# Layer A's products in the wide form, c spread by DMA, layer B's tokens in the order of t mod 4

## The chip, the cores and the metric

The kernel runs on one core of one Trainium2 chip. The metric is the time of one execution in microseconds on the device; the time of a kernel is the median of several executions. One execution of each kernel is also profiled: the profile gives every instruction of the five engines (PE for matmuls, PEld for the loads of PE's weights, DVE for vectors, ACT for activations, POOL for general work) and the transfers, which SP issues.

## The reference, cut to what matters

One sequence of 256 tokens (L), width 2048 (D), two layers. Layer A is a Mamba-2 mixer, layer B an attention over dilated windows. All inputs are float32.

```python
def reference(x, c, ada_w, ...):
    for layer in range(2):
        shift, scale, gate = split(silu(c) @ ada_w[layer] + ada_b[layer], 3)
        h = x * (1.0 + scale) + shift
        if layer == 0:            # layer A
            z, xBC, dt = split(h @ a_in_w, [4096, 4096 + 6144])
            xBC = silu(causal_conv4(xBC) + conv_b)
            xs, B, C = split(xBC)           # 64 heads of 64, 8 groups of 128
            y = ssd(xs, softplus(dt + dt_bias), A, B, C) + xs * D_skip
            y = rms_norm_by_group(y * silu(z)) * norm_g
            y = y @ a_out_w
        else:                     # layer B
            q, z = split(h @ b_in_w, [3072])
            for g, (window, dilation) in enumerate(((128, 1), (512, 4), (2048, 16))):
                # query t sees t, t - dilation, ..., t - window; ALiBi; 8 heads of 128
                o[g], lse[g] = attention(q[g], k_sh[g], v_sh[g])
            o = sum(o[g] * softmax(lse)[g]) * silu(z)
            y = o @ b_out_w
        x = layer_norm(2 ** 0.5 * x + (1 + gate) * y) * ln_g[layer] + ln_b[layer]
        if layer == 0:
            k_sh, v_sh = split(x @ kv_w, 2)
    return x
```

## The kernel before, in words

**Products.** Every weight comes as pieces of 128x1024 floats (512 KB, load_piece, L88, six buffers). A piece is split into two numbers of the type fp32r: ACT copies it (whi, L94), and DVE subtracts the copy from it (wlo, L95). The activations are split in the same manner into a high and a low part. A product is then high times high, high times low and low times high, all added up in PSUM.

There are three forms. In the *quad* form (cm_piece, L109 to L121) the result has the columns of the weight in its partitions: for each of the 16 blocks of 128 rows of the weight (kt) and each of four blocks of columns PE runs three matmuls over 256 tokens, L119, L120 and L121. In the *wide* form (cm_wide, L140) the high and the low activations lie side by side, so L151 multiplies the weights' high part with both at once over 512 columns, and L152 multiplies the low part with the high activations over 256. The result has two halves, joined by an ACT copy (L156) and a DVE add (L157). The third form (tm_piece, tm_mults, L172 to L174) has the tokens in the partitions and runs three matmuls over 512 columns of weight. Layer A's xs, B and C use the quad form, z the third; layer B's queries and part of its keys use the wide one.

**The start.** The two rows of c come by DMA into the tiles of z (sz, L415), PE multiplies them with a column of ones to spread them over the 128 partitions (L422), and ACT applies SiLU into cb_ (L423). The 96 columns of the modulation (scale, shift and gate of two layers, 16 blocks each) are tiles of 128x2048 (1 MB, ada_load, L230), and each is one DVE instruction, a product with cb_ that is summed along the row (ada_dot, L236). Once scale and shift of a block kt are there, ACT makes h of this block (L381, L382) and DVE its low part. The table of rows at L392 sets how the products that use the h blocks made so far stand between the blocks: seven pieces a row and two or four blocks h. Products begun here and finished later keep a partial sum in the tiles of y and sz (part).

**Layer A.** product (L326) computes xs, B and C by cm_quad, adds a partial sum if there is one (L344), and runs the causal convolution (conv, L298 to L307), which reads PSUM or the partial sum: one ACT instruction with bias and scale (L302), three DVE instructions (L305) and SiLU. stage1, stage2 and stage3 (from L528) do the scan of one group of heads each. The out projection, the residual and the layer norm follow (L657 to L699).

**Layer B.** x_tiles (L707) transposes the normed rows into xhi and xlo, the layer's activations; key and value products follow. u, the residual, is then multiplied with the layer norm's weight and given its bias by POOL (L766, L767), in 16 instructions of 128x512. attend (L785) runs for each of eight heads and two blocks b of 128 queries: three score matmuls, one a group (L795), with 128 keys for the first block and 256 for the second, the mask and slope by DVE (L797, L799), the softmax over all three groups together, transposes (L809), copies (L813, L815) and the products with the values (L819, L820). split_act (L841) splits the result for the last product.

**What sets the order.** The program is written in the order of the code and then re-ordered by a planner (price, graph, build, forward, backward, arrange): it has a price for every instruction and the transfers, works out when each could run, and writes each engine's queue anew, the issues on SP too. So the order on an engine is not that of the code.

Of the kernel before, what the change touches and what calls it, by code (L numbers as in the profile page):

```python
# [24 lines left out]
G = 8  # L25
# [21 lines left out]
CD, CA, NBIAS = 0, 256, 256 + 768  # L47
# [3 lines left out]
def trunk(ctx, tc, xT, x, c, par, cst, bias, lnrow, ada, wdt, win, wout, wkv, wk1, wbin, wbout, out):  # L51
    nc = tc.nc
    V, S, T, PO = nc.vector, nc.scalar, nc.tensor, nc.gpsimd
# [79 lines left out]
    def cm_quad(src, ahi, alo, rate=(0, 1), k0=0):  # L133
        ps = acc_pair()
        for q in range(k0 // 2, KT // 2):
            cm_piece(src, q, ps, ahi, alo, k0=k0)
            background(*rate)
        return ps

    def cm_wide(src, dst, rate=(0, 1)):  # L140


        ps = acc_pair()
        for q in range(KT // 4):
            hi, lo = (t.rearrange("p k n -> p (k n)").rearrange("p (k n) -> p k n", k=4)
                      for t in split(load_piece(src[q])))
            for k in range(4):
                kt = 4 * q + k
                for n in range(2):
                    c_ = slice(n * P, n * P + P)  # L150
                    T.matmul(ps[n], hi[:, k, c_], xp[:, kt], start=kt == 0, stop=False, skip_group_check=True)  # L151
                    T.matmul(ps[n][:, 0, :], lo[:, k, c_], xhi[:, kt, :], start=False, stop=kt == KT - 1,  # L152
                             skip_group_check=True)
            background(*rate)
        for n in range(2):
# [72 lines left out]
    def ada_load(pool, layer, kind, ct):  # L228
        raw = pool.tile([P, D], F32, name="araw", bufs=2)
        nc.sync.dma_start(raw, ada[layer, KIND.index(kind), ct])  # L230
        return raw

    def ada_dot(layer, kind, ct, raw):

        j = KIND.index(kind)
        V.scalar_tensor_tensor(raw, raw, 1.0, cb_, op0=ALU.mult, op1=ALU.mult,  # L236
                               accum_out=mod[layer][:, ct, j:j + 1])
# [31 lines left out]
    hp = act.tile([P, 2, KT, L], F32R, name="actT")  # L269
    hhi, hlo = hp[:, 0], hp[:, 1]  # L270

    with ExitStack() as cA:
# [14 lines left out]
        with ExitStack() as cS:  # L287
# [38 lines left out]
            def product(kind, g, pre=None):  # L326
# [13 lines left out]
                ps = cm_quad(src, hhi, hlo, rate=R, k0=k0)  # L340
                t = tiles(ps)
                if part is not None:
                    for w in range(2):
                        V.tensor_tensor(part[:, 2 * w:2 * w + 2, :], ps[w], part[:, 2 * w:2 * w + 2, :], op=ALU.add)  # L344
                    t = [part[:, n, :] for n in range(4)]
# [5 lines left out]
            with ExitStack() as c0:  # L351
# [68 lines left out]
                for i in range(4):  # L420
                    pc = mm.tile([P, 512], F32, name="acc")
                    T.matmul(pc, ones[:1, :], szt[i // 2][:1, i % 2, :], start=True, stop=True)  # L422
                    S.activation(cb_[:, 512 * i:512 * i + 512], pc, AF.Silu)  # L423
# [210 lines left out]
        def y_tiles(g):  # L634

            for i in range(4):
                ct = 4 * g + i
                if i % 2 == 0:
                    pt = aux.tile([P, 512], F32, name="aux").rearrange("p (i l) -> p i l", i=2)
                for b in range(2):  # L640
                    T.transpose(pt[:, i % 2, b * P:b * P + P], y[g][:, b, i * P:i * P + P], ident)
                w, hi = pv("normg")[:, ct:ct + 1], yhi[g // 4][:, ct % 16, :]
                S.activation(hi, pt[:, i % 2, :], AF.Copy, scale=w)
                V.scalar_tensor_tensor(ylo[g][:, i, :], pt[:, i % 2, :], w, hi.bitcast(F32),
                                       op0=ALU.mult, op1=ALU.subtract)
# [776 lines left out]
```

## Time and profile before

| | us |
|---|---|
| median of three executions | 1287.76 (1283.16 to 1289.54) |
| profiled execution | 1281.55 |
| span of its instructions | 1279.8 |
| granted TensorE clock in it, mean | 0.993 |

The span runs from the first to the last instruction of the profiled execution. Where the profile gives a group of instructions, the row has the line of the kernel, the engine, the operation and its tiles (out<-in), the shape, the count, the busy time and the mean of one, and behind the last bar the idle time of the engine just before them with what ended it. An engine's idle time costs nothing unless something else waits for it in turn.

### The profile page before, as it was taken

To read this page: it belongs to the slowest core of one execution; us is meant where nothing else is said; L and a number is where in the kernel's file an instruction comes from. 1 tells how busy PE (TensorE), PEld (TensorE's weight loads), DVE (VectorE), ACT (ScalarE), POOL (GpSimd) and SP (SyncE) were. 2 spreads that over 40 slices of the span, in tenths; PEclk is the share of its full clock that TensorE was granted. 3 is DMA by queue.
4 is the path that set the end of the run, shared out by engine and by line. 5 is a ranking of instruction groups with operands and counts; after the bars stand their busy time and mean duration, and the time that the engine had idled before them with its cause. 6 is when DMAs were issued, how large, how long until landed. Compare 5 with 4: busy or idle time off the path is not lost.

```text
span 1279.8 us, 19378 instructions
## 1 busy us (share of the span) xinstructions
PE 1239.4 (97%) x7386; PEld 1095.2 (86%) x7386; DVE 1039.2 (81%) x1457; ACT 696.6 (54%) x1027; POOL 33.3 (3%) x20
## 2 busy tenths in 40 slices
PE   6999999999999999999999899999999999999995
PEld 4978999899899999788888699888888888888884
DVE  6999978999998887978895799998745647848778
ACT  4644566868577767764333444444445645444551
POOL 0000000000000000000000135000000000000000
PEclk9999999999999999999999899999999999999998
DMA  9999967887785556578997688999866663453571
GB/s 372 422 422 422 384 216 268 314 276 247 240 300 191 173 159 203 162 258 269 400 376 218 222 315 308 396 420 395 299 191 193 211 185 115 147 183 107 155 266 66
DMA packets 80449, 334.82 MB, mean 262 GB/s; under 512 B 9090, under 2 KB 9314, under 8 KB 67684
## 3 DMA queue, kind: packets, MB, share of 16 engines
q1 hardware_dynamic: 80356, 333.58, 73.5%
q8 instruction: 58, 0.95, 0.3%
q14 instruction: 35, 0.29, 0.1%
HBM read 331.37 MB, written 2.18 MB: 261 GB/s over the span
## 4 chain that ended last, share of the span: by engine, by line
PE 78%; DMA 12%; DVE 7%; ACT 1%; issue 1%; SPq 0%; DVEq 0%; ACTq 0%
PE acc L151 12%; PE acc L174 11%; PE acc L173 11%; PE acc L172 11%; PE acc L152 6%; DMA raw<-in_win 6%; PE acc L119 6%; PE acc L121 6%; PE acc L120 6%; DMA araw<-in_ada 5%; DVE wlo L95 2%; PE py L589 1%; DVE araw L236 1%; PE aux L795 1%; PE po L819 1%
## 5 line engine op out<-in xcount | busy, mean ns | idle before, releaser
L95 DVE TENSOR_TENSOR wlo<-raw,whi 128x1024 fp32r<-128x1024 f32 x395 | 488.9, 1244 | 176.5 <-ACT whi L94 175.2
L94 ACT ACTIVATE whi<-raw 128x1024 fp32r<-128x1024 f32 x395 | 417.1, 1057 | 382.1 <-PE acc L174 178.6
L119 PE MATMUL acc<-actT,whi 128*128 128x256 f32 x960 | 273.6, 288 | 11.8 <-ACT actT L382 7.4
L173 PE MATMUL acc<-wlo,actT 128*128 128x512 f32 x704 | 276.4, 393 | 0.6 <-DVE wlo L95 0.6
L172 PE MATMUL acc<-whi,actT 128*128 128x512 f32 x704 | 274.8, 393 | 1.6 <-ACT whi L94 1.0
L121 PE MATMUL acc<-actT,wlo 128*128 128x256 f32 x960 | 270.5, 285 | 1.4 <-DVE wlo L95 1.4
L120 PE MATMUL acc<-actT,whi 128*128 128x256 f32 x960 | 271.3, 285 | 0.0
L151 PE MATMUL acc<-actT,whi 128*128 128x512 f32 x704 | 251.3, 398 | 0.0
L236 DVE SCALAR_TENSOR_TENSOR araw<-araw,cb__72 128x2048 f32<-128x2048 f32 x96 | 218.4, 2286 | 9.0 <-DMA araw<-in_ada 5.7
L152 PE MATMUL acc<-actT,wlo 128*128 128x256 f32 x704 | 201.8, 287 | 0.6 <-DVE wlo L95 0.6
L119 PEld LDWEIGHTS acc<-actT,whi 128*128 128x128 f32 x960 | 185.2, 194 | 15.7 <-ACT actT L382 9.0
L121 PEld LDWEIGHTS acc<-actT,wlo 128*128 128x128 f32 x960 | 184.0, 193 | 2.3 <-DVE wlo L95 2.0
L120 PEld LDWEIGHTS acc<-actT,whi 128*128 128x128 f32 x960 | 185.1, 193 | 0.3
L174 PE MATMUL acc<-whi,actT 128*128 128x512 f32 x448 | 175.1, 391 | 0.0
L172 PEld LDWEIGHTS acc<-whi,actT 128*128 128x128 f32 x704 | 131.9, 188 | 30.1 <-ACT whi L94 2.8
L151 PEld LDWEIGHTS acc<-actT,whi 128*128 128x128 f32 x704 | 132.2, 188 | 29.2
L173 PEld LDWEIGHTS acc<-wlo,actT 128*128 128x128 f32 x704 | 132.3, 188 | 27.5 <-DVE wlo L95 1.1
L152 PEld LDWEIGHTS acc<-actT,wlo 128*128 128x128 f32 x704 | 133.0, 189 | 1.9 <-DVE wlo L95 1.2
L174 PE MATMUL acc<-whi,ylo 128*128 128x512 f32 x256 | 100.8, 394 | 0.0
L174 PEld LDWEIGHTS acc<-whi,actT 128*128 128x128 f32 x448 | 84.1, 188 | 17.5 <-issue 0.5
L174 PEld LDWEIGHTS acc<-whi,ylo 128*128 128x128 f32 x256 | 48.1, 188 | 9.4
L305 DVE SCALAR_TENSOR_TENSOR cacc<-acc,prm,cacc 128x255 f32<-128x255 f32 (+2 forms) x96 | 43.7, 475 | 2.7 <-ACT cacc L302 2.3
(205 smaller groups left out, 1083.1 us busy)
## 6 DMA issues: line engine op xcount, KB each, us to landing
araw<-in_ada SPq DMA_DIRECT2D x96, 1024.0 KB, 7.2
raw<-in_win SPq DMA_DIRECT2D x160, 512.0 KB, 4.9
raw<-in_wkv SPq DMA_DIRECT2D x72, 512.0 KB, 4.9
raw<-in_wout SPq DMA_DIRECT2D x64, 512.0 KB, 5.6
raw<-in_wbin SPq DMA_DIRECT2D x64, 512.0 KB, 4.0
raw<-in_wk SPq DMA_DIRECT2D x24, 512.0 KB, 6.6
cbc<-cumd SPq DMA_DIRECT2D x16, 512.0 KB, 5.3
raw<-in_wbout SPq DMA_DIRECT2D x16, 512.0 KB, 4.3
```

The costliest lines, as they stand in the source:

```text
L94: S.activation(hi, raw, AF.Copy)
L95: V.tensor_tensor(lo, raw, hi.bitcast(F32), op=ALU.subtract)
L119: T.matmul(o, hi[:, k, c_], ahi[:, kt, :], start=first, stop=False, skip_group_check=True)
L120: T.matmul(o, hi[:, k, c_], alo[:, kt, :], start=False, stop=False, skip_group_check=True)
L121: T.matmul(o, lo[:, k, c_], ahi[:, kt, :], start=False, stop=kt == k1 - 1, skip_group_check=True)
L151: T.matmul(ps[n], hi[:, k, c_], xp[:, kt], start=kt == 0, stop=False, skip_group_check=True)
L152: T.matmul(ps[n][:, 0, :], lo[:, k, c_], xhi[:, kt, :], start=False, stop=kt == KT - 1, skip_group_check=True)
L172: T.matmul(ps[b], h_, hi[:, k, :], start=kt == k0, stop=False)
L173: T.matmul(ps[b], h_, lo[:, k, :], start=False, stop=False)
L174: T.matmul(ps[b], l_, hi[:, k, :], start=False, stop=kt == k1 - 1)
L236: V.scalar_tensor_tensor(raw, raw, 1.0, cb_, op0=ALU.mult, op1=ALU.mult, accum_out=mod[layer][:, ct, j:j + 1])
L305: V.scalar_tensor_tensor(acc[:, o:], ps[:, :L - o], w[:, j:j + 1], acc[:, o:], op0=ALU.mult, op1=ALU.add)
```

## The change

It has these parts.

- The quad form is gone from product: xs 1 to 7 and B/C 2, 4 and 6 run as two halves of the wide form each, on weights laid out for it (wsub, pieces of four kt and 256 columns). The high and low parts of h lie side by side for it (hp). Where there is no partial sum, the halves are joined into a new tile ct, four buffers, from which conv reads; where there is one, both halves are added to it.
- c is spread by four DMAs that read it 128 times over into cb_; ACT applies SiLU in place. The first scale and shift column are loaded and multiplied in two halves each.
- Layer B's tokens stand in the order of t mod 4 (0, 4, 8, ..., 1, 5, ...): x_tiles reads PSUM with a stride, split_act at the end writes back in the order of t. The groups with dilation 4 and 16 then see keys of their own block of 128 only, and their scores and values are computed for that block. Bias and mask come from a table of 2 x 768 columns, kept in cb_.
- POOL's sixteen instructions on u are DVE's.
- y_tiles is grouped in pairs, and the planner counts 3 us more for a DMA that writes to DRAM.

```diff
-    def cm_wide(src, dst, rate=(0, 1)):
+    def cm_wide(src, both, high, rate=(0, 1), k0=0):
         ps = acc_pair()
-        for q in range(KT // 4):
+        for q in range(k0 // 4, KT // 4):
...
-                    T.matmul(ps[n], hi[:, k, c_], xp[:, kt], start=kt == 0, stop=False, skip_group_check=True)
-                    T.matmul(ps[n][:, 0, :], lo[:, k, c_], xhi[:, kt, :], start=False, stop=kt == KT - 1,
+                    T.matmul(ps[n], hi[:, k, c_], both[:, kt], start=kt == k0, stop=False, skip_group_check=True)
+                    T.matmul(ps[n][:, 0, :], lo[:, k, c_], high[:, kt, :], start=False, stop=kt == KT - 1,
...
-        V.scalar_tensor_tensor(raw, raw, 1.0, cb_, op0=ALU.mult, op1=ALU.mult,
-                               accum_out=mod[layer][:, ct, j:j + 1])
+        to = mod[layer][:, ct, j:j + 1]
+        if (layer, ct) != (0, 0) or kind == "gate":
+            V.scalar_tensor_tensor(raw, raw, 1.0, cb_, op0=ALU.mult, op1=ALU.mult, accum_out=to)
+            return
+        half = mod[0][:, j, 2:3]
+        for c_, o in ((slice(0, D // 2), half), (slice(D // 2, D), to)):
+            V.scalar_tensor_tensor(raw[:, c_], raw[:, c_], 1.0, cb_[:, c_], op0=ALU.mult, op1=ALU.mult, accum_out=o)
+        V.tensor_tensor(to, to, half, op=ALU.add)
...
-                ps = cm_quad(src, hhi, hlo, rate=R, k0=k0)
-                t = tiles(ps)
-                if part is not None:
-                    for w in range(2):
-                        V.tensor_tensor(part[:, 2 * w:2 * w + 2, :], ps[w], part[:, 2 * w:2 * w + 2, :], op=ALU.add)
-                    t = [part[:, n, :] for n in range(4)]
+                t = []
+                for w in range(2):
+                    ps = cm_wide(wsub[2 * WSUB.index((kind, g)) + w], hp, hhi, rate=R, k0=k0)
+                    for n in range(2):
+                        if part is None:
+                            t.append(p0.tile([P, L], F32, name="ct", bufs=4))
+                            S.activation(t[-1], ps[n][:, 1, :], AF.Copy)
+                            V.tensor_tensor(t[-1], ps[n][:, 0, :], t[-1], op=ALU.add)
+                        else:
+                            t.append(part[:, 2 * w + n, :])
+                            for i in range(2):
+                                V.tensor_tensor(t[-1], ps[n][:, i, :], t[-1], op=ALU.add)
...
-                for i in range(2):
-                    row = szt[i].rearrange("p b n -> p (b n)")[:1]
-                    nc.sync.dma_start(row, c[:, 1024 * i:1024 * i + 1024])
+                for i in range(4):
+                    bcast(cb_[:, 512 * i:512 * i + 512], c, 512 * i)
+                    S.activation(cb_[:, 512 * i:512 * i + 512], cb_[:, 512 * i:512 * i + 512], AF.Silu)
                 fetch()
                 fetch()
                 fetch_x(0)
                 nc.sync.dma_start(adab_, par[:, :NB])
-                for i in range(4):
-                    pc = mm.tile([P, 512], F32, name="acc")
-                    T.matmul(pc, ones[:1, :], szt[i // 2][:1, i % 2, :], start=True, stop=True)
-                    S.activation(cb_[:, 512 * i:512 * i + 512], pc, AF.Silu)
...
+            pt = pt.rearrange("p (j r) -> p r j", r=4)
...
-                PO.tensor_tensor(u[b][:, cs_], u[b][:, cs_], lnr[0], op=ALU.mult)
-                PO.tensor_tensor(u[b][:, cs_], u[b][:, cs_], lnr[1], op=ALU.add)
+                V.tensor_tensor(u[b][:, cs_], u[b][:, cs_], lnr[0], op=ALU.mult)
+                V.tensor_tensor(u[b][:, cs_], u[b][:, cs_], lnr[1], op=ALU.add)
...
+                for g in (1, 2):
+                    T.matmul(pq[:, (g - 1) * P:g * P], qq[:, g, i, cb], kk[hq][:, g, i, cb], start=True, stop=True)
+                T.matmul(pq[:, 2 * P:], qq[:, 0, i, cb], kk[hq][:, 0, i, :], start=True, stop=True)
...
+            T.matmul(po, v[:, 0, 0, ci], pT[:, :, 2, :], start=True, stop=False)
+            T.matmul(po, v[:, 0, 1, ci], pT[:, :, 3, :], start=False, stop=False)
+            for b in range(2):
+                for g in (1, 2):
+                    T.matmul(po[:, b * P:b * P + P], v[:, g, b, ci], pT[:, b, g - 1, :], start=False, stop=b == 1 and g == 2)
```

How the planner's queues change, at three places. The first is SP's queue at the start of the program, with what was issued before: sz are the rows of c, araw columns of the modulation, adab their biases, xt a tile of x, raw pieces of weights.

```order
L415 DMA sz<-in_c 1x1024 x2
L230 DMA araw<-in_ada 128x2048
L419 DMA adab<-in_par 128x96
L230 DMA araw<-in_ada 128x2048
L365 DMA xt<-in_xT 128x512
L230 DMA araw<-in_ada 128x2048
L88 DMA raw<-in_win 128x1024
L230 DMA araw<-in_ada 128x2048
L88 DMA raw<-in_win 128x1024 x5
```

The same place in the changed kernel's queue of SP, where cb_ is the spread c:

```order
L67 DMA cb__72<-in_c 128x512 x4
L232 DMA araw<-in_ada 128x1024 x4
L379 DMA xt<-in_xT 128x512
L91 DMA raw<-in_win 128x1024
L433 DMA adab<-in_par 128x96
L91 DMA raw<-in_win 128x1024
L232 DMA araw<-in_ada 128x2048 x2
L91 DMA raw<-in_win 128x1024
L232 DMA araw<-in_ada 128x2048
L91 DMA raw<-in_win 128x1024 x2
```

The spread c now stands first, the first two columns follow as four halves, adab has moved behind the tile of x and one piece, and a second piece stands ahead of the third and fourth column.

The second place is the middle of the first stage on SP, where pieces and columns alternate; before, from the 22nd row on:

```order
L88 DMA raw<-in_win 128x1024 x4
L230 DMA araw<-in_ada 128x2048 x4
L88 DMA raw<-in_win 128x1024 x2
L365 DMA xt<-in_xT 128x512
L88 DMA raw<-in_win 128x1024 x4
L230 DMA araw<-in_ada 128x2048 x4
```

The changed kernel's SP, from its 24th row on:

```order
L232 DMA araw<-in_ada 128x2048
L91 DMA raw<-in_win 128x1024 x2
L232 DMA araw<-in_ada 128x2048
L91 DMA raw<-in_win 128x1024 x2
L232 DMA araw<-in_ada 128x2048
L379 DMA xt<-in_xT 128x512
L91 DMA raw<-in_win 128x1024 x2
L232 DMA araw<-in_ada 128x2048
```

Bursts of four columns and six pieces have become one column and two pieces in turn.

The third place is PE's queue in the first pieces of the product xs 1; the tiles of the result are acc_2032 and acc_2033, actT_86 holds h, and whi_2036 and wlo_2037 are the split piece. Before, from the second block of columns on:

```order
L119 MATMUL acc_2032<-actT_86,whi_2036 128x256
L120 MATMUL acc_2032<-actT_86,whi_2036 128x256
L121 MATMUL acc_2032<-actT_86,wlo_2037 128x256
L119 MATMUL acc_2033<-actT_86,whi_2036 128x256
L120 MATMUL acc_2033<-actT_86,whi_2036 128x256
L121 MATMUL acc_2033<-actT_86,wlo_2037 128x256
```

The same place on PE in the changed kernel:

```order
L146 MATMUL acc_2032<-actT_86,whi_2036 128x512
L147 MATMUL acc_2032<-actT_86,wlo_2037 128x256
L146 MATMUL acc_2033<-actT_86,whi_2036 128x512
L147 MATMUL acc_2033<-actT_86,wlo_2037 128x256
```

Three matmuls of 256 columns have become one of 512 and one of 256, and both result tiles are filled in turn by the same piece.

More of the change, by code (lines that the diff above doesn't have):

```diff
@@ L45, with trunk @@
 CI, CT, CM, NCONST = 0, 128, 256, 512
-CD, CA, NBIAS = 0, 256, 256 + 768
+NKEY = 768
+WSUB = [("xs", g) for g in range(1, G)] + [("bc", g) for g in (2, 4, 6)]
+CD, CA, NBIAS = 0, NKEY, 2 * NKEY
 @with_exitstack
-def trunk(ctx, tc, xT, x, c, par, cst, bias, lnrow, ada, wdt, win, wout, wkv, wk1, wbin, wbout, out):
+def trunk(ctx, tc, xT, x, c, par, cst, bias, lnrow, ada, wdt, win, wsub, wout, wkv, wk1, wbin, wbout, out):
     nc = tc.nc
-    V, S, T, PO = nc.vector, nc.scalar, nc.tensor, nc.gpsimd
+    V, S, T = nc.vector, nc.scalar, nc.tensor
     cons = ctx.enter_context(tc.tile_pool(name="cons", bufs=1))
@@ L229, in ada_load @@
         raw = pool.tile([P, D], F32, name="araw", bufs=2)
-        nc.sync.dma_start(raw, ada[layer, KIND.index(kind), ct])
+        n = 2 if (layer, ct) == (0, 0) and kind != "gate" else 1
+        for i in range(n):
+            c_ = slice(D // n * i, D // n * i + D // n)
+            nc.sync.dma_start(raw[:, c_], ada[layer, KIND.index(kind), ct][:, c_])
         return raw
@@ L634, in y_tiles @@
         def y_tiles(g):
[L636 to L645, printed above, removed]
+            for j in range(0, 4, 2):
+                pt = aux.tile([P, 512], F32, name="aux").rearrange("p (i l) -> p i l", i=2)
+                for i in range(2):
+                    for b in range(2):
+                        T.transpose(pt[:, i, b * P:b * P + P], y[g][:, b, (j + i) * P:(j + i) * P + P], ident)
+                for i in range(2):
+                    ct = 4 * g + j + i
+                    w, hi = pv("normg")[:, ct:ct + 1], yhi[g // 4][:, ct % 16, :]
+                    S.activation(hi, pt[:, i, :], AF.Copy, scale=w)
+                    V.scalar_tensor_tensor(ylo[g][:, j + i, :], pt[:, i, :], w, hi.bitcast(F32),
+                                           op0=ALU.mult, op1=ALU.subtract)
         def y_ahead(q):
```

95 lines of the change are left out of this document (46 added, 49 removed).

## The prediction

> **What bounds the kernel now.** I read the span and the busy shares first, then the chain of work that ended last, then the busy time stage by stage, and only then single rows.
>
> ```profile
> span 1279.8 us, 19378 instructions
> PE 1239.4 (97%) x7386; PEld 1095.2 (86%) x7386; DVE 1039.2 (81%) x1457; ACT 696.6 (54%) x1027; POOL 33.3 (3%) x20
> PE 78%; DMA 12%; DVE 7%; ACT 1%; issue 1%; SPq 0%; DVEq 0%; ACTq 0%
> ```
>
> PE is busy 1239.4 of 1279.8 us, so the idle time that a better order could win is 40.4 us in all; everything else has to come from giving PE less to do. The view of busy time by stretch (length, then busy time of PE, PEld, DVE, ACT and POOL, the granted clock, the DMA share, GB/s) shows where those 40 us lie:
>
> ```profile
> 20.00:60.00 40.00, 38.70 (x256) 36.01 (x256) 35.93 (x38) 23.56 (x35) 0.00 (x0) 1.00 1.02 422
> 60.00:100.00 40.00, 38.56 (x207) 32.37 (x207) 37.36 (x40) 21.68 (x31) 0.00 (x0) 1.00 1.02 423
> 100.00:145.00 45.00, 43.53 (x315) 40.68 (x314) 42.20 (x45) 18.19 (x23) 0.00 (x0) 1.00 1.02 422
> 147.00:545.00 398.00, 395.62 (x2740) 365.62 (x2740) 350.17 (x566) 285.71 (x473) 0.00 (x0) 1.00 0.69 233
> 720.00:745.00 25.00, 18.74 (x135) 17.84 (x134) 23.50 (x43) 12.08 (x17) 6.39 (x4) 0.86 0.76 251
> 745.00:815.00 70.00, 68.86 (x541) 66.65 (x541) 68.22 (x66) 32.19 (x39) 26.69 (x12) 1.00 0.89 333
> 815.00:1064.00 249.00, 249.00 (x1255) 211.46 (x1254) 174.48 (x191) 120.53 (x156) 0.00 (x0) 1.00 0.79 278
> 1064.00:1112.00 48.00, 48.00 (x295) 42.77 (x294) 41.64 (x98) 24.27 (x49) 0.00 (x0) 1.00 0.35 104
> ```
>
> Three stages can be told apart. Up to 145 us the transfers run at 422 GB/s without a pause and PE waits for them. In the state-space stage (147 to 545) PE waits 2.4 us of 398, but DVE is at 88%. Around the hand-over to layer B (720 to 815) PE waits 6.3 and then 1.1 us, with DVE at 94% and 97%. From 815 on PE is full.
>
> **A: c spread by DMA, first columns in halves.** The start, as the timelines of PE, DVE and ACT have it (start, length, instruction, then idle time ahead and its releaser):
>
> ```profile
> 2.27 7.16 PE L422 MATMUL acc<-sz,ones 1*128 1x512 f32 x8 [2.27 <-DMA sz<-in_c]
> 16.87 0.79 PE L119 MATMUL acc<-actT,whi 128*128 128x256 f32 x2 [7.43 <-ACT actT L382]
> 19.69 0.80 PE L119 MATMUL acc<-actT,whi 128*128 128x256 f32 x2 [2.03 <-ACT whi L94]
> 20.92 0.80 PE L119 MATMUL acc<-actT,whi 128*128 128x256 f32 x2 [0.43 <-ACT whi L94]
> 21.51 1.48 PE L120 MATMUL acc<-actT,whi 128*128 128x256 f32 x6
> 22.79 0.41 PE L121 MATMUL acc<-actT,wlo 128*128 128x256 f32 x1
> ```
> ```profile
> 10.10 2.29 DVE L236 SCALAR_TENSOR_TENSOR araw<-araw,cb__72 128x2048 f32<-128x2048 f32 x1 [3.30 <-ACT cb__72 L423]
> ```
> ```profile
> 21.98 0.59 ACT L381 ACTIVATE htmp<-xt,mod 128x256 f32<-128x256 f32 x1
> 22.60 0.42 ACT L382 ACTIVATE actT<-htmp 128x256 fp32r<-128x256 f32 x1
> ```
>
> Today c arrives as two rows, PE spreads it until 9.4, and the first dot can start only at 10.10. The change removes the spreading and puts 1.05 MB on the stream ahead of everything: at 422 GB/s that is 2.5 us, from a first byte near 2.3 us (where the c rows land today) to about 4.9. The four half columns (2.1 MB) are in at 9.9, the last half dot (half of 2.29) ends at 11.1, and then adab decides, now issued behind the x tile and one piece (0.26 + 0.52 + 0.05 MB, 2.0 us): 11.9, with the small adds 12.3, and with 0.59 + 0.42 us of ACT the first product starts near 13.4 instead of 16.87. The second h needs two more columns and a piece (2.6 MB, 6.3 us, in at 18.2), two dots of which one is late (2.3), the add and the two ACT steps: 21.7 instead of 23.0. PE has by then done the 24 matmuls that the first h allows, where today 13 stand ahead of 23.0. At the 0.12 us a matmul worked out under B, the lead is 1.3 + 12 x 0.12 = 2.7 us.
>
> ```profile
> araw<-in_ada SPq DMA_DIRECT2D x96, 1024.0 KB, 7.2
> lnr<-in_lnrow SPq DMA_DIRECT2D x8, 256.0 KB, 6.5
> ```
>
> The new issue order also mixes columns and pieces finely (7 pieces to 4 columns) where today 4 columns come in one burst, 4.2 MB or 10 us without a piece. In the three stretches from 20 to 145 PE idles 1.3, 1.4 and 1.5 us; I expect a third of this 4.2 to go, 1.3 us. Together I take **-4**. Bounds: were all 4.2 us to go beside a first lead of 2.7, -7. The spread tile of lnr, also read 128 times over from one row, took 6.5 us to land (median, 256 KB); if c lands as slowly, its four tiles in line, the 2.5 us of stream are a loss and little of the lead is left: up to +4.
>
> **B: wide products.** 512 groups of three 256-wide matmuls become 512 pairs of one 512-wide and one 256-wide. Both forms stand in the trace; starts of the same line, six triples apart, and three and thirteen pairs apart:
>
> ```profile
> 300.39 0.28 PE L119 MATMUL acc<-actT,whi 128*128 128x256 f32 x1
> ...
> 302.55 0.28 PE L119 MATMUL acc<-actT,whi 128*128 128x256 f32 x1
> ```
> ```profile
> 839.87 0.39 PE L151 MATMUL acc<-actT,whi 128*128 128x512 f32 x1
> ...
> 840.91 0.39 PE L151 MATMUL acc<-actT,whi 128*128 128x512 f32 x1
> ```
> ```profile
> 1029.73 0.40 PE L151 MATMUL acc<-actT,whi 128*128 128x512 f32 x1
> ...
> 1034.32 0.40 PE L151 MATMUL acc<-actT,whi 128*128 128x512 f32 x1
> ```
>
> A triple takes 2.16 / 6 = 0.360 us (0.12 a matmul), a pair 1.04 / 3 = 0.347 or 4.59 / 13 = 0.353. I take the middle, 0.350: 512 x 0.010 = **-5.1**, bounds -3.6 and -6.7. The columns are the same, 768; what goes is one weight load and one start in three. It counts in full, since PE sets the end in this stage. The Trainium skill (TensorE: Matmul & The Clock Gate, "Wait — 56ns, not 53.3ns?") says that a stream of warm matmuls pays its columns at 2.4 GHz and some 2.5 ns each on top; by this a pair would save 2.5 ns and the whole term be an estimated -1.3, while the rows here show 7 to 13 ns.
>
> **C: attention.** Two groups now need only their own 128 keys. For scores and for values alike, 24 narrow (128) and 24 wide (256) fp32 matmuls become 32 and 16, and 72 transposes become 64.
>
> ```profile
> 1069.82 0.45 PE aux L795 x4
> ...
> 1080.89 0.44 PE po L819 x2
> ```
>
> These are steps of the chain of waits (start, length, engine, tile, records). Every fp32 matmul leaves two records; four of 128 columns take 0.45 us and two of 256 take 0.44, so a narrow matmul costs 0.22 us, a wide one 0.44, a transpose of 128 columns, one record, 0.11. Eight wide become eight narrow: 8 x 0.22 = 1.76, twice 3.5, and eight transposes are 0.9: **-4.4**, all of it on PE, which is full from 1064 to 1112. DVE loses half of its bias work there and has 6 us of slack already. Bounds -3.9 and -4.8, the 40 records read to 0.01 us.
>
> **D: weight and bias of the residual from POOL to DVE.** POOL's operations disturb DVE today; by groups, 725 to 815 and 600 to 720:
>
> ```profile
> L95 DVE TENSOR_TENSOR wlo<-raw,whi 128x1024 fp32r<-128x1024 f32 x27 | 41.4, 1540 | 0.0
> ```
> ```profile
> L95 DVE TENSOR_TENSOR wlo<-raw,whi 128x1024 fp32r<-128x1024 f32 x44 | 53.9, 1224 | 27.7 <-ACT whi L94 27.7
> ```
> ```profile
> L156 ACT ACTIVATE qq<-acc 128x256 f32<-128x256 f32 x32 | 12.0, 379 | 21.0 <-PE acc L152 21.0
> L157 DVE TENSOR_TENSOR qq<-acc,qq 128x256 f32<-128x256 f32 x32 | 13.4, 420 | 8.1 <-ACT qq L156 8.1
> L344 DVE TENSOR_TENSOR y<-acc,y 128x512 f32<-128x512 f32 x8 | 5.4, 685 | 0.6 <-PE acc L121 0.6
> L550 ACT ACT_TABLE_LOAD x10 | 12.8, 1283 | 0.2
> ```
>
> 27 x (1.540 - 1.224) = 8.5 us come off DVE just where PE waits for it, and 16 x 0.685 = 11 us come on where the new order places them, behind the last dot in 815 to 1064, of which DVE leaves 74.5 us free. PE waits 1.1 us in 745 to 815; waits shorter than the overlap of two records don't show as idle time, so I take **-2**, bounds -2.5 and +1 (the affine tiles collide with the splits). The gap while the layer norm ends is the same work in both kernels and counts nothing.
>
> **E: evictions in the state-space stage.** Twelve halves without a begun part get 24 ACT copies and 24 DVE adds, where conv read PSUM directly; eight with one get 32 adds of 256 for 8 of 512. DVE: 24 x 0.42 + 32 x 0.42 - 8 x 0.685 = +18 us, from 350 to 368 of 398 (93%); ACT: 24 x 0.379 + 6 more table loads x 1.283 = +17 of 112 free. PE's cover for this is its four result banks; it loses 2.4 us there now. An engine at 93% of the load that feeds PE will be late a little more often: **+2**, bounds 0 and +8 (a wait of 0.42 at each of the 20 halves). The strided reads and writes of the new token order cost 0 to +2 at the first tiles and nothing behind them, since DVE and ACT work ahead there; I take 0.
>
> **Sum.** -4 - 5.1 - 4.4 - 2 + 2 = -13.5. The profiled execution took 1281.55 us, span and 1.75 around it, so 1268.0 on its scale; it lies 6.2 below the median of the runs shown, and on the median's scale the result is **1274**.
>
> **The rivals.** *The stream is the bound, and c's megabyte is on it.* Up to 145 us all is paid at 422 GB/s; 1.05 MB more makes 2.5 us, and if the lead is lost in it (the 6.5 us of lnr speaks for it, that PE now starts 16.87 us in speaks against), A becomes +3 and the sum -6.5: 1281. *Banks handed over late* (the slower one): each half must be copied and added before its two banks are used again, 0.379 + 2 x 0.42 = 1.22 us behind whatever DVE has queued. This decides once DVE runs late by more than a half's own time, which is 32 pairs or 11 us in a whole product, but 8 pairs or 2.8 us in bc 4 and bc 6; with DVE at 93% that is possible. If all 20 halves paid it, +24.4 in place of +2 makes +9: 1297. Against it speaks the row of L157: ahead of the same add DVE idled 8.1 us for ACT's copy, so there it is the add that waits, not the bank for the add. *The wide form does nothing*: a pair carries a triple's 768 columns and costs its 0.360; the sum is -8.4, 1279.4. The rule named under B would put it at 1278. *More of everything*: A at -7, B at -6.7, E at 0 make -20.1: 1268.
>
> **How the numbers follow.** Forecast, 1269 to 1280: 0.58. Stream: 0.14, half of it within 0.5%. Late banks: 0.12, of it 0.04 within 0.5%, since not all halves need pay. No gain by width: 0.06. More: 0.10, down to 1263. 0.5% of the median, about what a measurement of this kernel can tell from no change, is 6.4 us, so faster means below 1281.3 and slower above 1294.2. Faster: 0.58 - 0.02 for the forecast's edge + 0.07 + 0.06 + 0.10 = 0.79; same: 0.02 + 0.07 + 0.04 = 0.13; slower 0.08. The range 1263 to 1287 leaves out the late banks and the tail of the large gain.
>
> **What would show it.** A: the first product near 13.4 and the second h near 21.7; c landing near 5; less than 4.2 us of PE idle from 20 to 145. B: starts 0.350 apart in the products of xs, 512 of them. C: PE's work in layer B 4.4 us less. D: wlo back near 1224 ns throughout 725 to 815. E: PE idle in the state-space stage under 5 us with DVE near 93%. The prediction is wrong if the first product comes after 16.9, if PE idles over 10 us between 147 and 545 (late banks), or if a stage that I hold unchanged, the layer norm's gap or the end behind the last product, differs by over 2 us.

## The result, and the profile after

| | before | after |
|---|---|---|
| median, us | 1288.35 (1283.16 to 1289.54) | 1266.5 (1265.38 to 1268.27) |
| profiled execution, us | 1281.55 | 1265.38 |
| its span, us | 1279.8 | 1263.6 |

The ratio is 0.9839 (95% interval 0.981 to 0.9869): 21.9 us less by the medians, inside the range of the prediction (1263 to 1287), but more than its 14 and below the 1269 to 1280 that it called its forecast. The profiled executions lie 16.2 apart. The other 5.7 go with the scatter of the kernel before: in the longest comparison below, 19 of its executions ran from 1281.11 to 1293.08, and the one with a profile stood near their lower end. In that series the six executions with a mean granted clock of 0.992 or more took 1281.11 to 1285.49, the twelve with 0.989 or less 1285.44 to 1293.08. What follows explains the 16.2.

The span, the busy times and the chain by engine of the changed kernel:

```profile
span 1263.6 us, 18302 instructions
PE 1221.7 (97%) x6858; PEld 1063.5 (84%) x6858; DVE 1039.5 (82%) x1469; ACT 708.9 (56%) x1039; POOL 0.2 (0%) x4
PE 94%; DVE 3%; DMA 2%; ACT 1%; issue 0%; DVEq 0%; SPq 0%; ACTq 0%
```

PE is busy 17.7 us less, DVE as long as before. The transfers' share of the chain fell from 12% to 2%: the first stage is no longer held by them. The stretches that answer to those of before:

```profile
20.00:60.00 40.00, 37.83 (x259) 35.10 (x259) 36.12 (x39) 23.86 (x33) 0.00 (x0) 1.00 1.02 423
60.00:100.00 40.00, 40.00 (x229) 35.28 (x228) 38.27 (x41) 22.26 (x29) 0.00 (x0) 1.00 1.02 422
100.00:145.00 45.00, 45.00 (x334) 43.08 (x334) 43.77 (x48) 22.38 (x28) 0.00 (x0) 1.00 1.02 423
147.00:545.00 398.00, 397.03 (x2244) 342.06 (x2243) 368.50 (x630) 305.53 (x516) 0.00 (x0) 1.00 0.70 245
```

From 60 to 145 PE waits nothing at all, at the same 422 GB/s. From 147 to 545 DVE stands at 368.5 us, as worked out, and PE waits 1.0 us.

Five marks in PE's timeline cut every run into six stages that can be compared: the transposes of dt's rows, the last out product, the last key product in the quad form, the first score, and in the last matrix the first product that reads the tile hi (some 26 us behind the first product of this matrix). The first of them, before and after:

```profile
180.83 0.33 PE L453 MATMUL acc<-cc,dtrow 64*128 64x64 f32 x2
```
```profile
174.36 0.33 PE L463 MATMUL acc<-cc,dtrow 64*128 64x64 f32 x2
```

Lengths of the stages in us. I: start to dt's rows. II: to the last out product (the scan and the out product). III: to the last key product of the quad form, with the layer norm's gap. IV: to the first score. V: to this product of the last matrix. VI: to the end.

| run | I | II | III | IV | V | VI | span |
|---|---|---|---|---|---|---|---|
| before | 180.8 | 539.8 | 82.3 | 266.8 | 177.6 | 32.5 | 1279.8 |
| after | 174.4 | 533.4 | 82.3 | 266.9 | 173.9 | 32.8 | 1263.6 |
| e1 start alone | 174.8 | 544.7 | 82.3 | 268.7 | 176.9 | 32.4 | 1279.8 |
| e2 old start | 174.9 | 532.6 | 81.5 | 271.2 | 173.2 | 32.9 | 1266.3 |
| e3 quads | 174.1 | 538.9 | 82.1 | 271.3 | 173.9 | 32.9 | 1273.3 |
| e4 POOL | 173.9 | 532.7 | 89.8 | 271.5 | 173.9 | 32.8 | 1274.7 |
| e5 planner | 179.0 | 546.9 | 93.5 | 271.2 | 178.1 | 33.4 | 1302.0 |
| e6 affine alone | 180.6 | 545.2 | 81.1 | 266.9 | 177.7 | 32.5 | 1283.8 |
| e7 POOL late | 173.9 | 533.0 | 81.8 | 266.6 | 173.9 | 32.9 | 1262.1 |
| e8 halves, no spread | 173.5 | 533.5 | 82.2 | 271.2 | 173.9 | 33.0 | 1267.3 |
| e9 whole columns | 176.8 | 532.6 | 81.7 | 271.2 | 174.2 | 33.0 | 1269.5 |
| e10 wide alone | 178.2 | 534.8 | 89.7 | 271.3 | 178.5 | 33.3 | 1285.8 |
| e11 attention alone | 180.5 | 549.1 | 86.2 | 267.5 | 174.0 | 32.2 | 1289.4 |
| e12 both | 173.5 | 532.8 | 81.7 | 268.9 | 175.6 | 33.0 | 1265.6 |

The gain lies in three places: stage I -6.5, II -6.4, V -3.7; III and IV are what they were.

The start of the changed kernel, on PE, DVE and ACT, shows a first product at 17.39 us, later than before:

```profile
17.39 1.22 PE L122 MATMUL acc<-actT,whi 128*128 128x256 f32 x4 [17.39 <-ACT actT L396]
```
```profile
9.00 1.23 DVE L244 SCALAR_TENSOR_TENSOR araw<-araw,cb__72 128x1024 f32<-128x1024 f32 x1 [8.00 <-DMA araw<-in_ada]
...
12.67 1.23 DVE L244 SCALAR_TENSOR_TENSOR araw<-araw,cb__72 128x1024 f32<-128x1024 f32 x1
...
14.68 0.20 DVE L434 TENSOR_SCALAR adab<-adab 128x64 f32<-128x64 f32 x1 [0.59 <-DMA adab<-in_par]
```
```profile
6.33 1.99 ACT L429 ACTIVATE cb__72<-cb__72 128x512 f32<-128x512 f32 x3 [1.67 <-DMA cb__72<-in_c]
14.51 1.06 ACT L97 ACTIVATE whi<-raw 128x1024 fp32r<-128x1024 f32 x1 [6.19 <-DMA raw<-in_win]
15.47 0.58 ACT L395 ACTIVATE htmp<-xt,mod 128x256 f32<-128x256 f32 x1
15.97 1.06 ACT L97 ACTIVATE whi<-raw 128x1024 fp32r<-128x1024 f32 x1
16.94 0.40 ACT L396 ACTIVATE actT<-htmp 128x256 fp32r<-128x256 f32 x1
```

The issues, with the size of each and the median time from issue to landing:

```profile
araw<-in_ada SPq DMA_DIRECT2D x4, 512.0 KB, 7.4
cb__72<-in_c SPq DMA_DIRECT2D x4, 256.0 KB, 5.2
```

The four tiles of c land at 4.0, 6.3, 7.0 and 7.7 us, so c is complete 2.8 us later than the 4.9 worked out. All that stands behind it lands late by as much: the last half column at 12.6 instead of 9.9, adab at 14.7 instead of 11.9. The half dots keep up with their columns; the last starts at 12.67, when its column is there. The remaining 1.2 us are ACT's, which has a split of 1.06 us ahead of the first of the two steps that make h, and another between them. The second h is there at 24.4, not at 21.7.

### The profile page after: what moved, and what is told of

It is laid out like the page before. It is cut to its first block, busy times and chain, and to the rows that moved or that the text cites. A ratio compares the mean times of both kernels' runs of the same rounds, so it can differ in the third digit from the quotient of the medians.

```text
span 1263.6 us, 18302 instructions
## 1 busy us (share of the span) xinstructions
PE 1221.7 (97%) x6858; PEld 1063.5 (84%) x6858; DVE 1039.5 (82%) x1469; ACT 708.9 (56%) x1039; POOL 0.2 (0%) x4
## 4 chain that ended last, share of the span: by engine, by line
PE 94%; DVE 3%; DMA 2%; ACT 1%; issue 0%; DVEq 0%; SPq 0%; ACTq 0%
PE acc L146 23%; PE acc L173 14%; PE acc L171 14%; PE acc L172 14%; PE acc L147 11%; PE acc L122 4%; PE acc L123 4%; PE acc L124 4%; PE py L599 2%; DMA raw<-in_win 2%; PE po L833 1%; PE aux L809 1%; PE po L822 1%; PE aux L591 1%; PE aux L810 1%; PE aux L569 1%
## 5 line engine op out<-in xcount | busy, mean ns | idle before, releaser
L98 DVE TENSOR_TENSOR wlo<-raw,whi 128x1024 fp32r<-128x1024 f32 x395 | 480.7, 1222 | 164.1 <-ACT whi L97 162.6
L146 PE MATMUL acc<-actT,whi 128*128 128x512 f32 x1216 | 431.3, 399 | 0.0
L146 PEld LDWEIGHTS acc<-actT,whi 128*128 128x128 f32 x1216 | 228.2, 188 | 54.3
L240 DVE SCALAR_TENSOR_TENSOR araw<-araw,cb__72 128x2048 f32<-128x2048 f32 x94 | 214.8, 2286 | 8.2 <-DMA araw<-in_ada 7.8
L173 PE MATMUL acc<-whi,actT 128*128 128x512 f32 x448 | 174.9, 390 | 0.0
L122 PE MATMUL acc<-actT,whi 128*128 128x256 f32 x448 | 127.0, 291 | 19.4 <-ACT actT L396 18.4
L123 PE MATMUL acc<-actT,whi 128*128 128x256 f32 x448 | 127.9, 287 | 0.1
L122 PEld LDWEIGHTS acc<-actT,whi 128*128 128x128 f32 x448 | 86.8, 197 | 20.7 <-ACT actT L396 18.9
L123 PEld LDWEIGHTS acc<-actT,whi 128*128 128x128 f32 x448 | 87.7, 196 | 0.6 <-DVE actT L397 0.4
L558 ACT ACTIVATE seg<-cbc,cumT 128x128 f32<-128x128 f32 x128 | 40.3, 389 | 8.7 <-PE py L599 6.5
## 6 DMA issues: line engine op xcount, KB each, us to landing
raw<-in_win SPq DMA_DIRECT2D x96, 512.0 KB, 11.2
```

The lines of the kernel that those rows point to most:

```text
L98: V.tensor_tensor(lo, raw, hi.bitcast(F32), op=ALU.subtract)
L122: T.matmul(o, hi[:, k, c_], ahi[:, kt, :], start=first, stop=False, skip_group_check=True)
L123: T.matmul(o, hi[:, k, c_], alo[:, kt, :], start=False, stop=False, skip_group_check=True)
L146: T.matmul(ps[n], hi[:, k, c_], both[:, kt], start=kt == k0, stop=False, skip_group_check=True)
L173: T.matmul(ps[b], l_, hi[:, k, :], start=False, stop=kt == k1 - 1)
L558: S.activation(seg[:, hh, b, :], cbc[:, hh, b, :], AF.Relu, bias=cumT[:, b, h0 + hh:h0 + hh + 1], scale=-1.0)
```

## The experiments

Whoever undoes a part also lets the planner order everything anew. So each run is read by its stages, and the span alone says little.

**e1, the start alone**, on the kernel before:

```diff
-                    nc.sync.dma_start(row, c[:, 1024 * i:1024 * i + 1024])
+                    bcast(cb_[:, 512 * i:512 * i + 512], c, 512 * i)
...
-        nc.sync.dma_start(raw, ada[layer, KIND.index(kind), ct])
+            nc.sync.dma_start(raw[:, c_], ada[layer, KIND.index(kind), ct][:, c_])
```

> The kernel before with the new start alone (c spread by DMA, first two columns in halves); everything else as before. Theory 1: the start brings the whole gain up to the state-space stage, through the order of the stream and not through an earlier first product: first product at 17 to 18 us, PE idle from 60 to 145 us under 0.5 us instead of 2.9, profiled span near 1273 (6.5 less than 1279.8). Rival: that gain belongs to the new order as a whole, for which the wide products or the planner's new figure are needed; then the idle time stays at 2 to 3 us and the span is 1279 or more. The lead of 2.7 us that I had worked out would show as a first product near 13.4.

Median 1283.47 against 1285.78 (ratio 0.997, 0.9949 to 0.9991). The first product came at 17.6, dt's rows at 174.8: stage I has the whole gain, and PE idles 0.0 us from 60 to 145. But II is 4.9 us longer than before. PE's timeline and the stretches show it at the head of the scan:

```profile
229.02 3.68 PE L594 MATMUL py<-xd,seg 128*128 128x64 f32 x16 [2.08 <-DVE xd L566]
```
```profile
220.00:230.00 10.00, 7.56 (x35) 5.84 (x34) 7.87 (x12) 9.98 (x18) 0.00 (x0) 0.95 1.01 416
230.00:240.00 10.00, 10.00 (x44) 8.39 (x44) 8.22 (x11) 4.98 (x13) 0.00 (x0) 0.71 0.62 202
```

PE idles 2.4 us, and then the clock it is granted is 0.71 for the next 10 us, so the wait costs about twice its length. Theory 1 holds for stage I, and its span was wrong, since the time was lost again behind it.

**e2, the old start** in the changed kernel (the same lines the other way).

> The changed kernel with the old start (c by PE, whole columns). Theory 1: the idle time of PE between 60 and 145 us comes back (about 3 us, 6 us with the waits too short to show), span near 1270 (6.5 more than 1263.6). Rival: the stream stays as smooth, span under 1265.

Median 1266.78, like the changed kernel's 1266.5. PE's timeline has the first product 3.3 us later than the changed kernel's:

```profile
20.67 1.65 PE L122 MATMUL acc<-actT,whi 128*128 128x256 f32 x6 [11.18 <-ACT actT L387]
```

Dt's rows still come at 174.9, and PE idles 0.0 us from 60 to 145: without the new start the first stage is as short. So theory 1 falls as far as it made the start the cause. The planner's order is a mixed one here too, with at most four columns in a row once, near the beginning, and three later. Stage IV is 4.3 us longer.

**e5, the planner's figure alone**, on the kernel before; no instruction changes:

```diff
-        return 0.36, 0.0, None, _n(o) * list(o.ap)[0][1] * 4
+        return 0.36, 3.0 if str(o.bass_ap.tensor.space) == "DRAM" else 0.0, None, _n(o) * list(o.ap)[0][1] * 4
```

> The kernel before with the planner's 3 us for DMA writes to DRAM alone; no instruction is added or changed, only the order moves: on SP bursts of four columns in the first stage become one to three columns between the pieces. Theory (order): the waits between 40 and 145 us are those of the bursts, so PE's idle time from 60 to 145 falls from 2.9 us to under 1, the dt rows are transposed near 175 to 176 us instead of 180.8, and the span is 1273 to 1276. Rival (the parts): the waits go only with a new start or the wide products; 1279.8 stays.

Median 1303.03 against 1287.13, ratio 1.0134 (1.0107 to 1.016): with the same work, the order alone is worth 16 us. Stage I gained 1.9 us, not 5, and PE still idles 1.9 us from 60 to 145; the order is mixed at first but ends with columns in runs of 3, 4, 4 and 4. The loss is in II, 7.1 us, in III, 11.2, and in IV, 4.4.

**e9, whole columns** in the changed kernel:

```diff
-        n = 2 if (layer, ct) == (0, 0) and kind != "gate" else 1
-        for i in range(n):
...
+        nc.sync.dma_start(raw, ada[layer, KIND.index(kind), ct])
```

> The changed kernel with the first two columns loaded and multiplied whole; c still spread by DMA. The planner's order of SP is then mixed finely up to about the 20th column, and ends the first stage with columns in runs of 3, 4 and 4. Theory (bursts make the waits): PE without idle time from 60 to about 100 us, and then 0.7 us or more at each run of four, 1.5 to 3 us in all by the dt rows (176 to 177.5 instead of 174.4). Rival (the mixed order has nothing to do with it, the changed parts have): dt rows at 174 to 175.

Median 1270.43. Dt's rows at 176.8. The stretches show PE's waits of 0.8 and 1.1 us, and its timeline where two of them lie:

```profile
60.00:100.00 40.00, 39.21 (x215) 33.76 (x214) 37.55 (x43) 22.30 (x30) 0.00 (x0) 1.00 1.02 422
100.00:145.00 45.00, 43.90 (x319) 41.34 (x318) 42.38 (x46) 21.60 (x27) 0.00 (x0) 1.00 1.02 424
```
```profile
98.63 0.51 PE L171 MATMUL acc<-whi,actT 128*128 128x512 f32 x1 [0.54 <-ACT whi L97]
116.54 0.39 PE L122 MATMUL acc<-actT,whi 128*128 128x256 f32 x1 [0.50 <-ACT whi L97]
```

Counted across a tile of x that may stand inside, the runs are of 3, 4, 4 and 4 columns. They land their last column at 95.0, 113.0, 131.0 and 148.8 us, and each time PE waits 2 to 4 us later for the pieces that come behind it: at 97 to 99, 115 to 117, 134.6 and 152.6.

That settles stage I. All kernels whose columns come singly, in twos and at most in threes, apart from one early run of four in e2, have dt's rows at 173.5 to 174.9 (after, e1, e2, e3, e4, e7, e8, e12); those that end with a run of three and two or three runs of four at 176.8 to 179.0 (e5, e9, e10); those with five runs of four, at 180.5 to 180.8 (before, e6, e11).

**e8, halves without the spread** in the changed kernel: c by PE as before, the first columns in halves.

> The changed kernel with c spread by PE again, but the first columns still in halves: 1 MB less on the stream. Theory (the spread delays the first columns by some 1.5 us and its stream time is then missing): first product at 14.5 to 16 us instead of 17.4, and 1 to 3 us less at the dt rows (171 to 173.5 instead of 174.4). Rival (the first stage ends when its bytes and products allow, whatever the first product does, as the old start showed): dt rows at 174 to 175.

Median 1269.48. The first product came at 15.8, dt's rows at 173.5, 0.9 us earlier: the upper edge of the theory's range. A first product 1.6 us earlier was worth 0.9. The spread of c costs about this much. Stage IV has the 4.3 us again.

**e3, quad products** in the changed kernel:

```diff
-                    ps = cm_wide(wsub[2 * WSUB.index((kind, g)) + w], hp, hhi, rate=R, k0=k0)
+                ps = cm_quad(src, hhi, hlo, rate=R, k0=k0)
```

> The changed kernel with xs and B/C in the quad form again, all else as changed. Theory: the wide form is worth its pairs alone, 512 x 0.010 = 5.1 us: span 1268 to 1269.5, PE idle from 147 to 545 about as now (1 us). Rival: with the evictions gone from DVE and ACT (18 and 17 us less) the state-space stage waits less, as I had priced at 2 us: span near 1266.5. Second rival: the wide form also took waits away there (1.3 us less seen): near 1270.5.

Median 1274.9, ratio to the kernel before 0.9899 (0.9864 to 0.9935) where the changed kernel has 0.9839. Stage II took 538.9, 5.6 more, about what the pairs alone ask for, with 0.75 us more of idle time of PE in it; IV, which has none of these products, took 4.4 more. So the span of 1273.3 is not the price of the quads alone.

**e10, wide products alone**, on the kernel before (the core of the diff).

> The kernel before with the wide products alone; on SP runs of three and four columns stay in the second half of the first stage. Theory: PE's own work shrinks by 5 us, the dt rows come at 177 to 180 (some waits of the bursts stay), the rest depends on what the new order makes of the scan's head and of the key products, where undoing parts has cost 0 to 12 us. From the wide form alone span 1273 to 1276; with a bad place in the order more. Rival (a pair costs a triple): PE's work from 147 to 545 as before and no part of the gain.

Median 1289.54 against 1286.7 (0.9998 to 1.004). I and II are 2.6 and 5.0 shorter, as expected, and III and IV 7.4 and 4.5 longer: all given back in layer B, which the edit does not touch.

**e4, POOL again** in the changed kernel, and **e6, the affine alone** on DVE in the kernel before:

```diff
-                V.tensor_tensor(u[b][:, cs_], u[b][:, cs_], lnr[0], op=ALU.mult)
...
+                PO.tensor_tensor(u[b][:, cs_], u[b][:, cs_], lnr[0], op=ALU.mult)
...
```

In e6 the same lines go the other way.

> The changed kernel with POOL doing the residual's weight and bias again. Theory: worth nothing, since the stretch from the last out product to the end of the key products was 82.27 us before and 82.26 after, so wlo was not what PE waited for: span within 0.7 of 1263.6, though wlo's subtraction takes near 1540 ns again beside POOL. Rival (my step D): 2 us more, 1265.6, with the stretch at 84.

> The kernel before with the residual's weight and bias on DVE alone; the order of the first stage keeps its bursts. Theory (room): PE waited hardly 1 us for wlo beside POOL there, so the stretch from the last out product to the last key product stays at 82.3 us and the span within 1.5 of 1279.8. Rival (my step D): 2 us less. Second rival (what undoing it in the changed kernel cost): 8 to 11 us less.

e4: median 1276.38, ratio 0.9911 (0.9883 to 0.994), a span 11.1 above the changed kernel's. Both its theory and its rival were far too low. Of this, III has 7.5 us; IV is 4.6 longer, as in runs that have no POOL beside DVE (e2, e3, e8, e9). e6: 1283.58 against 1287.13 (0.9963 to 0.9997), with III at 81.1, 1.2 less than before, and 5.4 us lost at the head of the scan. DVE's groups in stage III, before, after and in e4:

```profile
L95 DVE TENSOR_TENSOR wlo<-raw,whi 128x1024 fp32r<-128x1024 f32 x23 | 36.7, 1597 | 0.0
L236 DVE SCALAR_TENSOR_TENSOR araw<-araw,cb__72 128x2048 f32<-128x2048 f32 x10 | 22.8, 2280 | 0.0
```
```profile
L240 DVE SCALAR_TENSOR_TENSOR araw<-araw,cb__72 128x2048 f32<-128x2048 f32 x14 | 32.0, 2285 | 1.1 <-DMA araw<-in_ada 1.1
L98 DVE TENSOR_TENSOR wlo<-raw,whi 128x1024 fp32r<-128x1024 f32 x24 | 29.2, 1219 | 2.7 <-ACT whi L97 2.6
```
```profile
L98 DVE TENSOR_TENSOR wlo<-raw,whi 128x1024 fp32r<-128x1024 f32 x23 | 35.4, 1545 | 0.0
L240 DVE SCALAR_TENSOR_TENSOR araw<-araw,cb__72 128x2048 f32<-128x2048 f32 x13 | 32.9, 2534 | 0.4 <-DMA araw<-in_ada 0.4
```

Before, POOL slowed wlo to 1597 ns, and DVE was full (0.0 idle), but only 10 columns of layer 1 stood in this stage, which just fitted. The new order puts 13 or 14 there. Without POOL 14 fit; beside POOL 13 don't. What PE waits for in e4 from 707 to 797 us (total, times, longest):

```profile
PE acc L124 <- DVE wlo L98: 4.4, 4, 2.4
```

The other runs with POOL in this stage say the same: e1 10 columns, 82.3; e11 12, 86.2; e10 13, 89.7; e5 15, 93.5. Each column over 10 costs 1.9 to 2.5 us, about its own dot (2.28).

**e7, POOL late**: POOL's 16 instructions, through one tile that comes free only behind the modulation:

```diff
-            lnr = [pl.tile([P, 512], F32, name=f"lnr{i}", bufs=2) for i in range(2)]
...
+            lnr = pc2.tile([P, 512], F32, name="lnr", bufs=1)
...
```

> The changed kernel with POOL doing the residual's weight and bias, but through one tile that is free only after the modulation of layer B, so not beside the key products. Theory (POOL slows DVE where DVE is full): the stretch of the key products is back at 82 to 83 us, wlo's subtraction at 1220 ns, span 1263 to 1267. Rival (the order, not POOL's company, made 1274.7): 1272 or more, with the stretch at 87 or more.

Median 1265.89, span 1262.1. The first row is DVE's wlo in stage III, the second POOL's first pair:

```profile
L98 DVE TENSOR_TENSOR wlo<-raw,whi 128x1024 fp32r<-128x1024 f32 x24 | 29.1, 1224 | 2.2 <-ACT whi L97 2.2
```
```profile
997.19 3.56 POOL L781 TENSOR_TENSOR u<-u,lnr 128x512 f32<-128x512 f32 x2 [996.74 <-DMA lnr<-in_lnrow]
```

The same engine with the same work, 280 us later, costs nothing, and stage III holds 14 columns here too: it is POOL's company of a full DVE that cost 7.5 us, not POOL's work as such. Beside POOL, from 997 to 1057 us, wlo's subtraction is slowed here as well, to 1421 ns instead of 1225, but DVE idles 22.1 us there.

**e11, attention alone**, on the kernel before (token order, masks and the core of attend).

> The kernel before with layer B's token order and attention alone. Theory: from the first score to the first product of the last matrix 173.9 us instead of 177.6, 3.7 less, the first stage with its bursts as before (dt rows at 180.5 to 181), span 1275 to 1277 unless the new order adds waits elsewhere. Rival (the strided accesses cost time): 1278 or more, with the key products' stretch above 82.3.

Median 1288.73 against 1286.7 (1.0001 to 1.004), so no gain. Stage V is 174.0, 3.6 less, as expected. Lost are 3.9 in III (12 columns beside POOL) and 9.3 in II, at the head of the scan again; its stretches there:

```profile
230.00:240.00 10.00, 6.07 (x27) 4.69 (x25) 9.90 (x16) 9.82 (x17) 0.00 (x0) 0.74 0.83 343
240.00:250.00 10.00, 10.00 (x34) 7.97 (x35) 6.16 (x7) 5.53 (x11) 0.00 (x0) 0.57 0.62 226
```

Whether the strided accesses cost anything isn't told by this run, since the 12 columns explain stage III; the changed kernel, with the same accesses, has 82.3 there.

**e12, the two variants together** (e7 and e8).

> The changed kernel with the two variants together that came out no slower: halves without the spread of c by DMA, and the residual's weight and bias by POOL, late. Theory: the first stage 0.9 us shorter (dt rows at 173.5) and the key products without waits, span 1260.5 to 1262.5. Rival (any new order may bring waits between 790 and 880 us back, as in three of the variants): 1265 to 1267.

Median 1267.28, span 1265.6: stage I as short as hoped, IV and V 3.7 us longer than the changed kernel's. The rival was right. Neither this nor e7 (1263.89 to 1268.05 in four executions) is told apart from the changed kernel.

## Why the prediction was right, point by point

**The number.** 1266.5 lies in the stated range, but in the part that the prediction called *more of everything* (1268) and gave 0.10, and not in the forecast's own 1269 to 1280. Some of it is luck: A came by another way, and the errors of D and E cancel. One of the prediction's own signs of being wrong was seen, a first product after 16.9.

**What bounds it.** Right: the gains lie where PE waited for the stream and where PE was given less to do.

**A, -4; measured -6.5, by another way.** The step that failed is the lead of 2.7 us: "the first product starts near 13.4". It started at 17.39. The spread of c, 2.8 us slower than at the 422 GB/s assumed, and the splits on ACT, 1.2 us, took the lead. The prediction had named the slow spread as its upper bound, from lnr's 6.5 us; c's tiles took 5.2. (In the sum of the lead, 24 less 13 matmuls are 11, not 12, which is 0.1 us.) e2 shows that the lead is not needed. What paid was the smaller part of the term, the mixing of columns and pieces, mis-sized at 1.3: no wait is left from 60 to 145 us. The 4.2 us idle that I read from the stretches were too few, since a record ends later than the next one could start (0.28 us long, 0.12 apart, in the rows of B), so each wait shows 0.16 us shorter than it is. That the mixing pays is shown by e9 and by the grouping of all runs. e1 gets it from the new start alone and e2 without it, so the start is not needed for it; what makes the planner mix is not shown.

**B, -5.1; right.** The pairs in one product of xs now start 4.51 / 13 = 0.347 us apart:

```profile
394.62 0.40 PE L146 MATMUL acc<-actT,whi 128*128 128x512 f32 x1
...
399.13 0.39 PE L146 MATMUL acc<-actT,whi 128*128 128x512 f32 x1
```

By 0.347, 512 pairs would save 6.7 us. Over the whole of stage II, which holds all 512, the starts of pairs that follow each other lie 0.3524 us apart in the mean and 0.350 in the median, those of e3's triples 0.3606 and 0.360, which makes 4.2 to 5.1 us. The stage is 5.6 shorter than in e3. The rival that a pair costs a triple falls. So does, for this case, what the Trainium skill (TensorE: Matmul & The Clock Gate, "Wait — 56ns, not 53.3ns?") would give, an estimated 2.5 ns a pair; the trace shows 8 to 10 in the stage and 13 in this product.

**C, -4.4; measured -3.7.** Right in kind, sized a little high: twice in the table, after and e11.

**D, -2; measured 0 to -1.2, and -7.5 in the new order.** Stage III didn't move from before to after; alone (e6) the edit shortens it by 1.2 us, and undone in the changed kernel (e4) it costs 7.5. The step that failed is that PE waits there for wlo: it hardly did with 10 columns. I had read DVE's full queue as a price; it was a limit that only the next column would cross, and the new order crosses it.

**E, +2; measured 0 or below.** DVE's 368 us were right to the microsecond, and PE waited less than before. The fear that 93% makes late banks is refuted, and so is the slower rival: from 147 to 545 PE idled 1.0 us in all.

**The sum.** -6.5 - 6.4 - 3.7 and +0.4 elsewhere are the 16.2 of the profile; my -13.5 was 2.7 short: A gave 2.5 more and B's stage 1.3 more, C 0.7 less, the rest 0.4 less, and the 2 us of D and E cancel. The other 5.7 us between the medians come from carrying the profile over: I added 6.2 us, the distance of before's profile from its median, and the changed kernel's is 1.1.

**What the terms don't add up to.** Alone, the start, the affine, the wide form and the attention give 1283.5, 1283.6, 1289.5 and 1288.7: hardly anything; the planner's figure gives 1303.0, a loss. The pairs of y_tiles were not run alone. In the kernel before each new order ran into one of two tight places, the head of the scan or DVE beside POOL (e5 and e10 lost in stage IV as well). Together the parts shrink and empty these places. That they could cancel was not among my rivals. Still open are the 4.3 us in stage IV of seven runs, in which PE waits there for DVE's wlo (3.2 us in e8) and in the changed kernel and e7 not at all, with seemingly the same columns (18 in e7, 18 in e8). Open too is why the head of the scan waits in some orders and not in others, and why the executions of the kernel before, and of its variants, scatter more. The waits at the head of the scan with a lower clock behind them, seen in e1, e6 and e11, could be that scatter; no execution of the kernel before with such a wait was traced.

## What to carry to other kernels

Where a planner orders the queues, every edit is two edits: its own work and a new order, and the second can be the larger (16 us from one planner figure). Count what an edit takes from the engine that sets the end, since that part held in every run, and look for the places where a second engine is exactly full, because there the next instruction costs its whole length. Mix large transfers that feed one step with those that feed another as finely as their use is mixed; bursts turn a stream that is fast enough on average into waits.

## What the runs showed of the hardware

A DMA that reads one row 128 times over slowed the stream. The transfers of the first 30 us in 40 slices, in GB/s, in the kernel before and in the changed one:

```profile
GB/s 0 0 11 109 262 426 415 369 451 415 415 314 273 328 407 399 431 426 437 426 399 421 404 431 421 410 426 410 418 404 451 413 467 404 426 437 426 426 426 423
```
```profile
GB/s 0 0 117 178 309 249 202 216 366 380 333 399 431 421 415 415 412 418 424 434 448 415 426 437 404 442 399 448 437 437 377 421 410 431 453 431 442 382 404 426
```

In the three slices from 3.75 to 6 us, with c's tiles on their way, the changed kernel moved 202 to 249 GB/s, and the kernel before, without them, 369 to 426. The slices ahead of these are low in both.

POOL beside DVE slowed DVE: wlo's subtraction took 1545 to 1597 ns on average instead of 1219 (in e4 from 735 to 790 us 1215 in the median and up to 2310), and a dot in e4 2534 instead of 2285, up to 3.4 us, though in the kernel before 2280. POOL's own pairs of instructions took 2.8 to 5.6 us in e4 and 3.2 to 3.6 in e7.

A short wait of PE at the head of the scan could cost more than its length: after 2.4 us (e1) and 3.9 us (e11) of idle time within 10 us the granted clock of the next 10 us was 0.71 and 0.57. In e6 1.1 us went with 0.76 and 0.73, while 0.7 us in the kernel before and 0.8 in e10 left it at 1.00; what sets it is not shown.
